# An expert layer in float32: the last weight tile split like the others, the final product moved from VectorE to GpSimd and ScalarE

## Chip, cores and metric

The kernel runs on one core of a Trainium2 chip. The metric is the device time of one execution in microseconds.

## What is computed

The program is one layer of a hybrid encoder in float32 for 2048 tokens of width 1024: a gated linear attention and a multi-head latent attention side by side, an output projection with residual, and then a mixture of 64 SwiGLU experts in 8 groups (one group per token, two experts of that group), with a final norm. The change touches the experts alone. Of the reference, that is:

```python
def expert_block(args):
    xb, e = args
    hdn = jax.nn.silu(xb @ w_gate[e]) * (xb @ w_up[e])
    return hdn @ w_down[e]
...
h = h + hier_moe(rmsnorm(h, ffn_norm[l]), ...)      # each token: two experts, weighted
return rmsnorm(h, final_norm)[:, N_META:]
```

Gate and up are 1024 x 512 for each expert, down is 512 x 1024: 6.3 MB of weights an expert, 403 MB in all.

## The kernel before

Up to about 1200 us the program makes the attention, the residual rows (kept in the output tensor) and the tables of the router. Then follow 64 blocks, one for each expert, taken so that neighbours belong to different groups. A block has room for 112 rows (tokens).

**Weights.** An expert's weights come as six tiles of 128 x 2048, 1 MB each: g0, g1 (gate), u0, u1 (up), d0, d1 (down). SP loads them into six raw buffers (`raw`). ScalarE (ACT) rounds a tile to `hi` in the matmul's reduced float32 (class `Weight`, `high`, line 1324), VectorE (DVE) takes `lo = raw - hi` (`low`, line 1330). There are four `hi` and four `lo` buffers, so a tile's `hi` and `lo` wait for the matmuls of the tile four places earlier. A product is then three matmuls (`mm3`, line 133): hi by hi, lo by hi, hi by lo. Five tiles go this way; the sixth, d1, is in `NATIVE` (line 44): it is used as plain float32 straight from `raw` (`down_whole`, line 1611), with a plain copy `hc` of its half of the hidden rows.

**One block on each engine,** by the names of the plan:
- TensorE (PE): `M_g0`, `M_g1`, `TH` (transposes of the hidden rows h of the block before), `M_u0`, `M_u1`, `TX0`, `TX1` (transposes of the next block's x), `M_d0`, `M_d1a`, `M_d1`.
- DVE: `lo_*`; `PROD`, the product h of silu(gate) and up; `HL` and `XL0`, `XL1`, the low parts of h and x; `Y0`, `Y1`, which add the down product in PSUM to the gathered base rows b and give z (two halves); `L`, the final product o = z * ss * g.
- ACT: `hi_*`; `HH`, `HC`, `XH0`, `XH1` (copies from PSUM); `SILU`; `SQ`, which squares z and sums to ss; `GM`, which makes the row g of norm weights.
- GpSimd (POOL): `GA` (gather of x for a later block), `GB` (gather of b, the rows' present values, from the output), `RT` (the root: two steps on ss, line 1651), `SO` (scatter of o to the output).

ss and g are such that a row's first visit leaves z as it is and its second visit normalizes it.

**Order.** `moe_plan` (line 1427) lays the order out with a list of operations, each with an engine, a cost in us and what it waits for; the order on each engine is then fixed. Gathers and scatters are indirect DMAs that POOL issues; weights are loaded by SP in the order in which the `hi` are planned. z has three buffers (`ZB`), b and o two each.

Of the kernel before, what the change touches and what calls it, by code (L numbers as in the profile page):

```python
# [8 lines left out]
F32 = mybir.dt.float32  # L9
# [3 lines left out]
AF = mybir.ActivationFunctionType  # L13
OP = mybir.AluOpType
# [4 lines left out]
P = 128  # L19
# [4 lines left out]
L = SEQ + META  # L24
# [267 lines left out]
def phase_g(tc, nc, a, zf, zv, hg, qd, qrd, kv, ident, ones, eps, z_rest, z_close, **_):  # L292
    late = ExitStack()
    with ExitStack() as ctx:
# [1132 lines left out]
def moe_plan():  # L1427


    W = 12 * 0.216  # L1430
    ops = {}

    def op(n, b, eng, cost, *deps):
        ops[n] = (b, eng, cost, deps)

    n = len(TILES)
    for i, t in enumerate(TILES):
        b, k = -(t[0] == "d"), i - HB
        old = ("M_" + TILES[k % n], -(k // n))
        op("hi_" + t, b, "A", 1.95, old)  # L1440
        op("lo_" + t, b, "V", 2.4, ("hi_" + t, 0), old)

    def ready(t):
        return [("lo_" + t, 0)] if t in TILES else []

    def cost(t):
        return W if t in TILES else W * 4 / 3

    for i, t in enumerate(("g0", "g1", "u0", "u1")):
        op("M_" + t, 0, "T", cost(t), *ready(t), *([(f"XL{i}", 1)] if i < 2 else []), *{0: [("PROD", 1)], 2: [("SILU", 1)]}.get(i, []))  # L1450
    op("M_d0", -1, "T", cost("d0"), *ready("d0"), ("HL", 0), ("Y0", 1), ("Y1", 1))
    op("M_d1a", -1, "T", cost("d1") / 2, *ready("d1"), ("HC", 0))
    op("M_d1", -1, "T", cost("d1") / 2, *ready("d1"), ("HC", 0))
    op("TH", -1, "T", 0.4, ("PROD", 1))
    op("HH", -1, "A", 0.43, ("TH", 0), ("M_d1", 2))
    if NATIVE:
        op("HC", -1, "A", 0.36, ("TH", 0), ("M_d1", 2))
    op("HL", -1, "V", 0.54, ("HH", 0), ("HC", 0))
    op("GA", 2, "G", 2.1, ("TX1", 0))
    op("GD", 2, "Q", 4.5, ("GA", 0))  # L1460
    for j in range(2):
        op(f"TX{j}", 1, "T", 0.4, ("GD", 1))
        op(f"XH{j}", 1, "A", 0.43, (f"TX{j}", 0), (f"M_u{j}", 0))
        op(f"XL{j}", 1, "V", 0.6, (f"XH{j}", 0))
        op(f"Y{j}", -1, "V", 0.7, (("M_d1a", "M_d1")[j], 0), ("Y0", 0) if j else ("BQ", 0), *([] if j else [("L", ZB)]))
    op("SILU", 0, "A", 0.68, ("M_g1", 0), ("PROD", 1))
    op("PROD", 0, "V", 0.72, ("M_u1", 0), ("SILU", 0), ("TH", 0))
    op("GB", -1, "G", 1.7, ("Y1", BB), ("OQ", 8))
    op("BQ", -1, "Q", 5.0, ("GB", 0))
    op("SQ", -1, "A", 1.3, ("Y1", 0), ("OQ", OB))  # L1470
    op("RT", -1, "G", 1.3, ("SQ", 0))
# [26 lines left out]
    late, t = {}, 0.0  # L1498
# [22 lines left out]
    while any(todo.values()):  # L1521
        best = None
        for k, v in todo.items():
            pick = None
            for q in v[:1 if k == "T" else 30]:
                if all(m in done for m in nodes[q][2]):
                    s = max([free[k]] + [done[m] + (LAG if nodes[m][0] != k else 0.07) for m in nodes[q][2]])
                    if k != "T":
                        s = max(s, late[q] - EARLY)
# [4 lines left out]
        s, q, k = best  # L1534
# [9 lines left out]
def phase_moe(tc, nc, a, ctx, ud, xlist, xexp, ident, ones, eps, rt, out, **_):  # L1544
    rp = rt["rp"]
    sp = ctx.enter_context(tc.tile_pool(name="e_s", bufs=2))
    p_g, p_t, xsb = rt["p_g"], rt["p_t"], rt["xs"]
    p_d = ctx.enter_context(tc.tile_pool(name="e_pd", bufs=2, space=PSUM))
    on = Ordered(tc)
    pools, made = rt["pools"], rt["made"]  # L1550
# [35 lines left out]
        on.scalar.activation(S.sg, S.p[0], AF.Silu, scale=S.rs)  # L1586

    def prod(S):
        S.h = sp.tile([BS, 4, P], F32, name="h", tag="h", bufs=1)
        on.vector.scalar_tensor_tensor(S.h.rearrange("s k p -> s p k"), S.p[1].rearrange("s (p k) -> s p k", k=4), S.grs,  # L1590
                                       S.sg.rearrange("s (p k) -> s p k", k=4), op0=OP.mult, op1=OP.mult)

    def turn(S):
        S.hn = 2 if NATIVE and S.e is not None else 4
        S.hh = sp.tile([P, 4, BS], F32R, name="hh", tag="hh", bufs=2)
        S.hl = sp.tile([P, 4, BS], F32R, name="hl", tag="hl", bufs=2)
        S.ph = p_t.tile([P, 4, BS], F32, name="pth", tag="t")
        for k in range(4):
            on.tensor.transpose(S.ph[:, k], S.h[:, k], ident[:BS, :BS])

    def hhi(S):
        on.scalar.copy(S.hh[:, :S.hn], S.ph[:, :S.hn])

    def hlo(S):
        on.vector.tensor_sub(S.hl[:, :S.hn], S.ph[:, :S.hn], S.hh[:, :S.hn].bitcast(F32))

    def hcopy(S):
        S.hc = sp.tile([P, 2, BS], F32, name="hc", tag="hc", bufs=2)
        on.scalar.copy(S.hc, S.ph[:, 2:])

    def down_whole(S, raw, hf):
        cs = slice(512 * hf, 512 * hf + 512)
        for k in range(2):
            on.tensor.matmul(S.d[hf], S.hc[:, k], raw[:, k, cs], start=False, stop=k == 1)
# [76 lines left out]

# [15 lines left out]
    for t in ("g0", "g1", "u0", "u1", "d0", "d1"):
        do["hi_" + t] = lambda S, g, t=t: hi(S, t, g)
# [6 lines left out]
    eng = {"T": on.tensor, "V": on.vector, "A": on.scalar, "G": on.gpsimd}  # L1715
# [23 lines left out]
    with tc.For_i(0, again, 1):  # L1739
        nx = nc.values_load(nxi[0:1, 0:1], min_val=0, max_val=NX)  # L1740
        with tc.For_i(0, nx, 1) as x:
# [8 lines left out]
            V = sp.tile([P, 2, NT, 4], F32, name="xV", tag="xV", bufs=1)  # L1750
# [8 lines left out]
            for k in range(2):  # L1759
                for t in range(NT):  # L1760
# [30 lines left out]
            for j in range(2):  # L1791
                w = Weight(nc, rp, *S.w["d", j]).high(rp, on.scalar).low(pools, 4 + j, on.vector).parts()
# [83 lines left out]
```

## Time and profile before

| | us |
|---|---|
| median of 3 runs (2433.43 to 2434.52) | 2434.23 |
| the profiled execution | 2433.11 |
| its span in the profile | 2431.1 |
| PE busy (share of the span) | 2343.4 (96%) |
| DVE busy | 1760.6 (72%) |
| ACT busy | 1385.0 (57%) |
| POOL busy | 831.3 (34%) |

Busy time is the time in which an engine's instructions ran, summed over the span. Matmuls are pipelined, so a PE that is busy throughout may still be waited for or wait a little; what a matmul takes is read from the distance between two starts. The three names `raw`, `hi` and `lo` in a row of the profile are the tiles above; `pg` and `pd` are the products in PSUM, `pt` and `pth` the transposes. Line 123 stands for every operation of the experts, as one helper records them all.

### The profile page before, as it was taken

To read this page: it belongs to the slowest core of one execution; us is meant where nothing else is said; L and a number is where in the kernel's file an instruction comes from. 1 tells how busy PE (TensorE), PEld (TensorE's weight loads), DVE (VectorE), ACT (ScalarE), POOL (GpSimd) and SP (SyncE) were. 2 spreads that over 40 slices of the span, in tenths; PEclk is the share of its full clock that TensorE was granted. 3 is DMA by queue.
4 is the path that set the end of the run, shared out by engine and by line. 5 is a ranking of instruction groups with operands and counts; after the bars stand their busy time and mean duration, and the time that the engine had idled before them with its cause. 6 is when DMAs were issued, how large, how long until landed. Compare 5 with 4: busy or idle time off the path is not lost. (4 is left out here: it accounts for less than half of the span.)

```text
span 2431.1 us, 35542 instructions
## 1 busy us (share of the span) xinstructions
PE 2343.4 (96%) x12897; PEld 1878.4 (77%) x12897; DVE 1760.6 (72%) x2755; ACT 1385.0 (57%) x2082; POOL 831.3 (34%) x676
## 2 busy tenths in 40 slices
PE   7999999899999999999699999999999999999997
PEld 7899997678789999989667767776777677777764
DVE  6334334677567676777778888888888888888885
ACT  5211103554356555555367777777777777777774
POOL 0000002622000212111234555555556545455553
PEclk9999999899999999999899999999999999999998
DMA  6212115555331212111599999999999999999994
GB/s 213 76 64 68 63 43 159 160 158 182 134 119 36 88 60 81 66 68 41 196 289 394 383 388 379 384 382 381 378 373 384 381 379 384 389 377 381 382 382 166
DMA packets 152960, 571.65 MB, mean 235 GB/s; under 512 B 28940, under 2 KB 71452, under 8 KB 103628
## 3 DMA queue, kind: packets, MB, share of 16 engines
q1 hardware_dynamic: 125612, 509.71, 56.5%
q0 software_dynamic: 24720, 50.91, 6.3%
q10 hardware_dynamic: 2448, 8.72, 1.2%
q8 instruction: 103, 1.69, 0.3%
q14 instruction: 77, 0.63, 0.1%
HBM read 529.71 MB, written 77.27 MB: 250 GB/s over the span
## 5 line engine op out<-in xcount | busy, mean ns | idle before, releaser
L123 DVE TENSOR_TENSOR lo<-raw,hi 128x2048 fp32r<-128x2048 f32 x317 | 720.7, 2285 | 67.5 <-ACT hi L123 61.7
L123 ACT CAST hi<-raw 128x2048 fp32r<-128x2048 f32 x318 | 607.6, 1911 | 275.1 <-PE pg L123 185.8
L123 PE MATMUL pg<-hi,xh 128*112 128x512 f32 x1024 | 434.3, 424 | 0.0
L123 PE MATMUL pg<-hi,xl 128*112 128x512 f32 x1024 | 407.6, 398 | 2.7 <-DVE xl L123 2.7
L123 PE MATMUL pg<-lo,xh 128*112 128x512 f32 x1024 | 401.8, 392 | 0.0
L123 POOL DMA_INDIRECT out_dram<-o,src x64 | 266.0, 4156 | 105.2 <-DVE hl L123 87.2
L123 POOL DMA_INDIRECT b<-out_dram,src x64 | 179.4, 2803 | 324.5 <-DVE z L123 324.0
L123 PEld LDWEIGHTS pg<-lo,xh 128*112 128x112 f32 x1024 | 180.5, 176 | 69.9 <-issue 15.1
L123 PEld LDWEIGHTS pg<-hi,xh 128*112 128x112 f32 x1024 | 179.4, 175 | 66.4 <-issue 13.9
L123 PE MATMUL pd<-raw,hc 128*112 128x512 f32 x512 | 230.1, 592 | 0.0
L123 PEld LDWEIGHTS pg<-hi,xl 128*112 128x112 f32 x1024 | 178.9, 175 | 61.8 <-DVE xl L123 3.3
L134 PE MATMUL ps<-uh,wh 128*128 128x256 f32 (+3 forms) x768 | 218.6, 285 | 0.9 <-ACT uh L222 0.9
L135 PE MATMUL ps<-ul,wh 128*128 128x256 f32 (+3 forms) x768 | 218.3, 284 | 0.0
L136 PE MATMUL ps<-uh,wl 128*128 128x256 f32 (+3 forms) x768 | 217.5, 283 | 0.0
L123 PEld LDWEIGHTS pd<-raw,hc 128*112 128x112 f32 x512 | 90.2, 176 | 103.8 <-issue 96.9
L134 PEld LDWEIGHTS ps<-uh,wh 128*128 128x128 f32 (+1 forms) x768 | 144.8, 189 | 1.6 <-ACT uh L222 1.3
L135 PEld LDWEIGHTS ps<-ul,wh 128*128 128x128 f32 (+1 forms) x768 | 144.7, 188 | 0.6 <-DVE ul L223 0.2
L136 PEld LDWEIGHTS ps<-uh,wl 128*128 128x128 f32 (+1 forms) x768 | 144.7, 188 | 0.1
L256 DVE COPY st<-ps 128x256 f32<-128x256 f32 (+1 forms) x64 | 27.0, 422 | 144.9 <-PE ps L136 144.9
L337 POOL TENSOR_SCALAR_AFFINE_SELECT mf<-ones 128x128 f32<-128x128 f32 x2 | 0.6, 302 | 378.8 <-PE ps L136 378.8
L123 DVE SCALAR_TENSOR_TENSOR o<-z,ss,g 112x1024 f32<-112x1024 f32 x64 | 82.2, 1284 | 55.6 <-POOL ss L123 53.2
L123 DVE TENSOR_TENSOR z<-pd,b 112x512 f32<-112x512 f32 x128 | 87.9, 686 | 45.3 <-PE pd L123 45.1
(2412 smaller groups left out, 5359.7 us busy)
## 6 DMA issues: line engine op xcount, KB each, us to landing
raw<-in_w_gate_dram SPq DMA_DIRECT2D x128, 1024.0 KB
raw<-in_w_up_dram SPq DMA_DIRECT2D x128, 1024.0 KB
raw<-in_w_down_dram SPq DMA_DIRECT2D x128, 1024.0 KB
x<-in_x_dram SPq DMA_DIRECT2D x32, 512.0 KB
zf<-st SPq DMA_DIRECT2D x85, 128.0 KB
hg<-x SPq DMA_DIRECT2D x16, 512.0 KB
x<-hg SPq DMA_DIRECT2D x16, 512.0 KB
out_dram<-x SPq DMA_DIRECT2D x16, 512.0 KB
```

Of the source, the lines that this page charges most:

```text
L123: return self.tc.keep_in_program_order(f(*args, **kw))
L134: nc.tensor.matmul(out, lh, rh, start=start, stop=False, **kw)
L135: nc.tensor.matmul(out, lh, rl, start=False, stop=False, **kw)
L136: nc.tensor.matmul(out, ll, rh, start=False, stop=stop, **kw)
L256: nc.vector.tensor_copy(st[:w, :n - o], ps[:w, :n - o])
L337: nc.gpsimd.affine_select(mf[:, :, hh], ob, pattern=[[CH, 2], [1, CH]], compare_op=OP.is_ge, fill=0.0, base=0, channel_multiplier=-1)
```

## The change

- `NATIVE` goes: d1 is split like the other tiles, its product is `mm3`, `hc` and `down_whole` go, and `HH` and `HL` take all four parts of h. `M_d1a` and `M_d1` wait for `lo_d1` and `HL`.
- h is kept as it is computed (112 x 512); the transposes of `TH` read it in steps of four, where before `PROD` wrote it in that order.
- The final product is in two: `ZG` on POOL multiplies g by z in place, `L` on ACT multiplies that by ss, a number for each row. In the last block DVE does it in one, as before.
- The plan has new costs; the due times of `L` and `SO` are later.

```diff
-NATIVE = ("d1",)
-TILES = tuple(t for t in ("g0", "g1", "u0", "u1", "d0", "d1") if t not in NATIVE)
+TILES = ("g0", "g1", "u0", "u1", "d0", "d1")
...
-    W = 12 * 0.216
+    W = 2.78
...
-    op("M_d1a", -1, "T", cost("d1") / 2, *ready("d1"), ("HC", 0))
-    op("M_d1", -1, "T", cost("d1") / 2, *ready("d1"), ("HC", 0))
+    op("M_d1a", -1, "T", cost("d1") / 2, *ready("d1"), ("HL", 0))
+    op("M_d1", -1, "T", cost("d1") / 2, *ready("d1"), ("HL", 0))
...
-    op("GB", -1, "G", 1.7, ("Y1", BB), ("OQ", 8))
+    op("GB", -1, "G", 2.6, ("Y1", BB), ("OQ", 8))
...
-    op("RT", -1, "G", 1.3, ("SQ", 0))
-    op("GM", -1, "A", 1.1, ("L", 2))
-    op("L", -1, "V", 1.3, ("RT", 0), ("GM", 0))
-    op("SO", -1, "G", 2.1, ("L", 0))
+    op("RT", -1, "G", 1.9, ("SQ", 0))
+    op("GM", -1, "A", 1.24, ("L", 2))
+    op("ZG", -1, "G", 2.1, ("Y1", 0), ("GM", 0))
+    op("L", -1, "A", 1.06, ("RT", 0), ("GM", 0), ("ZG", 0))
+    op("SO", -1, "G", 2.6, ("L", 0))
...
     def prod(S):
-        S.h = sp.tile([BS, 4, P], F32, name="h", tag="h", bufs=1)
-        on.vector.scalar_tensor_tensor(S.h.rearrange("s k p -> s p k"), S.p[1].rearrange("s (p k) -> s p k", k=4), S.grs,
-                                       S.sg.rearrange("s (p k) -> s p k", k=4), op0=OP.mult, op1=OP.mult)
+        S.h = sp.tile([BS, FE], F32, name="h", tag="h", bufs=1)
+        on.vector.scalar_tensor_tensor(S.h, S.p[1], S.grs, S.sg, op0=OP.mult, op1=OP.mult)
...
+    def weigh(S):
+        on.gpsimd.tensor_mul(S.g, S.g, S.z)
+
     def last_norm(S):
+        if S.i < NE - 1:
+            return on.scalar.activation(S.o, S.g, AF.Copy, scale=S.ss)
         on.vector.scalar_tensor_tensor(S.o, S.z, S.ss, S.g, op0=OP.mult, op1=OP.mult)
```

How this moves the instructions, in a block of the middle. On DVE, before, from behind the first z to the first xl (`lo0` is u0's, then u1, d0, g0, g1; `o` is L):

```order
L123 TENSOR_TENSOR lo0_17341<-raw_17306,hi_17308 128x2048
L123 TENSOR_TENSOR z_17326<-pd_17288,b_17244 112x512
L123 TENSOR_TENSOR lo1_17364<-raw_17318,hi_17320 128x2048
L123 TENSOR_TENSOR lo2_17376<-raw_17358,hi_17362 128x2048
L123 SCALAR_TENSOR_TENSOR o_17366<-z_17326,ss_17367,g_17343 112x1024
L123 TENSOR_TENSOR hl_17370<-pth_17371,hh_17369 128x224
L123 TENSOR_TENSOR lo3_17421<-raw_17400,hi_17402 128x2048
L123 TENSOR_TENSOR lo0_17455<-raw_17423,hi_17425 128x2048
L123 SCALAR_TENSOR_TENSOR h_17464<-pg_17378,grs_13958,sg_17453 112x128x4
L123 TENSOR_TENSOR xl_17428<-pt_17429,xh_17427 128x448
```

The same stretch of the changed kernel, from the lo of u0 on (then u1, d0, d1, g0, g1):

```order
L122 TENSOR_TENSOR lo2_17571<-raw_17537,hi_17539 128x2048
L122 TENSOR_TENSOR z_17569<-pd_17505,b_17457 112x512
L122 TENSOR_TENSOR lo3_17592<-raw_17565,hi_17567 128x2048
L122 TENSOR_TENSOR lo0_17618<-raw_17588,hi_17590 128x2048
L122 TENSOR_TENSOR lo1_17629<-raw_17624,hi_17626 128x2048
L122 TENSOR_TENSOR hl_17599<-pth_17600,hh_17598 128x448
L122 TENSOR_TENSOR lo2_17660<-raw_17645,hi_17647 128x2048
L122 SCALAR_TENSOR_TENSOR h_17688<-pg_17605,grs_13958,sg_17649 112x512
L122 TENSOR_TENSOR lo3_17691<-raw_17681,hi_17683 128x2048
L122 TENSOR_TENSOR xl_17653<-pt_17654,xh_17652 128x448
```

Between z and hl three `lo` now follow each other, where two and the final product stood; h stands between the `lo` of g0 and g1.

On POOL, before, a block from the root to the gather of b (`DMA` are the indirect ones: `out` SO, `xs` GA, `b` GB; a name in brackets is what is waited for):

```order
L123 TENSOR_SCALAR ss_20559<-ss_20559 112x1 [waits Activation_49]
L123 TENSOR_TENSOR ss_20559<-ss_20559,t_hx_14033 112x1 [waits Pool_49]
L123 DMA out_0_dram<-o_20558,src_6417 2048x1024 [waits DMASW5_49,DVE_49]
L123 DMA xs2_13832<-ud_73,src_6417 112x1024 [waits PE_49]
L123 DMA b_20892<-out_0_dram,src_6417 112x1024 [waits DMASW7_49,DMASW1_49,DVE_49]
```

And now:

```order
L122 DMA b_20228<-out_0_dram,src_6417 112x1024 [waits DMASW4_49,DMASW2_49,DVE_49]
L122 TENSOR_TENSOR g_20018<-g_20018,z_20014 112x1024 [waits Activation_49]
L122 TENSOR_SCALAR ss_20041<-ss_20041 112x1 [waits Activation_49]
L122 TENSOR_TENSOR ss_20041<-ss_20041,t_hx_14029 112x1 [waits Pool_49]
L122 DMA xs2_13832<-ud_73,src_6417 112x1024 [waits DMASW3_49,PE_49]
L122 DMA out_0_dram<-o_20040,src_6417 2048x1024 [waits Activation_49]
```

The product ZG (`g` by `z`) stands between the gather of b, which waits for the z before it on DVE, and the root; the gather of x is now ahead of the scatter.

On ACT, now, from `GM` on (`o,ss` from z is SQ, `o` from `g` and `ss` is L; the `hi` are d0, d1, g0, g1 and u0):

```order
L122 ACTIVATE g_18551<-gain_14086,t_first_14025,t_sec_14027 112x1024
L122 CAST hi_18568<-raw_18566 128x2048 [waits DMAHW1_49,DVE_49,PE_49]
L122 ACTIVATE o_18573,ss_18574<-z_18547 112x1024 [waits DMASW3_49,DVE_49]
L122 CAST hi_18604<-raw_18602 128x2048 [waits DMAHW2_49,PE_49,Activation_49]
L122 CAST hh_18576<-pth_18578 128x448 [waits PE_49]
L122 CAST hi_18625<-raw_18623 128x2048 [waits DMAHW3_49,PE_49,Activation_49]
L122 ACTIVATE sg_18627<-pg_18530,tab_6414 112x512
L122 ACTIVATE o_18573<-g_18551,ss_18574 112x1024 [waits Activation_49,Pool_49]
L122 CAST hi_18661<-raw_18659 128x2048 [waits DMAHW4_49,DVE_49,PE_49]
L122 CAST xh_18630<-pt_18632 128x448 [waits PE_49]
L122 CAST xh_18630<-pt_18633 128x448 [waits PE_49]
L122 CAST hi_18680<-raw_18678 128x2048 [waits DMAHW5_49,DVE_49,PE_49]
```

L stands ahead of the `hi` of g1 and waits for POOL.

## Rows read from the trace of the kernel before

**Rows 1.** Busy time by stage: us, PE, PEld, DVE, ACT, POOL, clock, DMA share, GB/s.
```profile
1800.00:2000.00 200.00, 200.00 (x863) 141.12 (x862) 173.32 (x131) 148.25 (x142) 110.79 (x54) 1.00 1.01 382
```
**Rows 2.** Groups of instructions by line: busy us, mean ns, idle before.
```profile
L123 ACT CAST hi<-raw 128x2048 fp32r<-128x2048 f32 x309 | 590.6, 1911 | 264.6 <-PE pg L123 175.3 <-DMA raw<-in_w_gate_dram 57.4 <-DMA raw<-in_w_up_dram 17.8
L123 ACT ACTIVATE o<-z 112x1024 f32<-112x1024 f32 x64 | 67.3, 1052 | 6.4 <-issue 6.4
...
L1177 POOL TENSOR_TENSOR x<-x,fge 128x1024 f32<-128x1024 f32 x14 | 33.5, 2390 | 85.0 <-PE pt L1162 72.7 <-PE pt__8088 L935 7.5 <-ACT qa L272 3.6
```
**Rows 3.** PE in order of time: start us, us, engine, operation.
```profile
1805.83 1.04 PE L123 MATMUL pt<-ident,xs 112*128 112x112 f32 x8
...
1809.46 3.60 PE L123 MATMUL pd<-raw,hc 128*112 128x512 f32 x8
...
1907.15 0.39 PE L123 MATMUL pg<-hi,xh 128*112 128x512 f32 x1
1907.38 0.39 PE L123 MATMUL pg<-lo,xh 128*112 128x512 f32 x1
```
**Rows 4.** DVE in order of time, one block of the expert stage.
```profile
1904.25 0.69 DVE L123 TENSOR_TENSOR z<-pd,b 112x512 f32<-112x512 f32 x1 [1.03 <-PE pd L123]
1904.86 2.28 DVE L123 TENSOR_TENSOR lo<-raw,hi 128x2048 fp32r<-128x2048 f32 x1
...
1907.66 2.28 DVE L123 TENSOR_TENSOR lo<-raw,hi 128x2048 fp32r<-128x2048 f32 x1
1910.68 2.29 DVE L123 TENSOR_TENSOR lo<-raw,hi 128x2048 fp32r<-128x2048 f32 x1 [0.74 <-ACT hi L123]
1913.76 1.29 DVE L123 SCALAR_TENSOR_TENSOR o<-z,ss,g 112x1024 f32<-112x1024 f32 x1 [0.79 <-POOL ss L123]
1914.96 0.38 DVE L123 TENSOR_TENSOR hl<-pth,hh 128x224 fp32r<-128x224 f32 x1
1915.26 4.48 DVE L123 TENSOR_TENSOR lo<-raw,hi 128x2048 fp32r<-128x2048 f32 x2
1919.66 1.16 DVE L123 SCALAR_TENSOR_TENSOR h<-pg,grs,sg 112x512 f32<-112x512 f32 x1
1920.65 1.15 DVE L123 TENSOR_TENSOR xl<-pt,xh 128x448 fp32r<-128x448 f32 x2
1922.81 0.69 DVE L123 TENSOR_TENSOR z<-pd,b 112x512 f32<-112x512 f32 x1 [1.01 <-PE pd L123]
```
**Rows 5.** POOL in order of time, the first from an earlier block.
```profile
1282.53 0.24 POOL L123 TENSOR_SCALAR ss<-ss 112x1 f32<-112x1 f32 x1
...
1908.01 2.79 POOL L123 DMA_INDIRECT b<-out_dram,src  x1 [4.57 <-DVE z L123]
1911.78 1.28 POOL L123 TENSOR_SCALAR ss<-ss 112x1 f32<-112x1 f32 x1 [0.98 <-ACT o L123]
1913.14 0.58 POOL L123 TENSOR_TENSOR ss<-ss,t_hx 112x1 f32<-112x1 f32 x1
1915.34 5.33 POOL L123 DMA_INDIRECT out_dram<-o,src  x1 [1.62 <-DVE hl L123]
1920.97 1.05 POOL L123 DMA_INDIRECT xs<-ud,src  x1 [0.30 <-issue]
```
**Rows 6.** DVE and POOL in order of time, before the expert stage.
```profile
1040.42 0.42 DVE L273 TENSOR_TENSOR ql<-qr,qh 128x256 fp32r<-128x256 f32 x1
1040.76 2.63 DVE L273 TENSOR_TENSOR qb__12397<-rr,qa 128x256 fp32r<-128x256 f32 x1
...
1040.73 2.39 POOL L1177 TENSOR_TENSOR x<-x,fge 128x1024 f32<-128x1024 f32 x1 [2.54 <-PE pt L1162]
```
**Rows 7.** A wait of PE in the first blocks: order of time, then busy by stretch.
```profile
1235.13 0.73 PE L123 MATMUL pg<-hi,xl 128*112 128x512 f32 x1 [2.69 <-DVE xl L123]
...
1232.44:1235.13 2.69, 0.00 (x1) 0.00 (x0) 2.69 (x5) 1.49 (x1) 1.96 (x1) 1.00 1.05 314
1235.13:1238.62 3.49, 3.48 (x8) 2.56 (x9) 3.41 (x7) 0.00 (x0) 0.00 (x0) 0.51 1.00 370
```

More of the change, by code (lines that the diff above doesn't have):

```diff
@@ L1439, in moe_plan @@
         old = ("M_" + TILES[k % n], -(k // n))
-        op("hi_" + t, b, "A", 1.95, old)
-        op("lo_" + t, b, "V", 2.4, ("hi_" + t, 0), old)
+        op("hi_" + t, b, "A", 1.92, old)
+        op("lo_" + t, b, "V", 2.3, ("hi_" + t, 0), old)
     def ready(t):
@@ L1446, in cost @@
     def cost(t):
-        return W if t in TILES else W * 4 / 3
+        return W
     for i, t in enumerate(("g0", "g1", "u0", "u1")):
@@ L1451, in moe_plan @@
     op("M_d0", -1, "T", cost("d0"), *ready("d0"), ("HL", 0), ("Y0", 1), ("Y1", 1))
-    op("M_d1a", -1, "T", cost("d1") / 2, *ready("d1"), ("HC", 0))
-    op("M_d1", -1, "T", cost("d1") / 2, *ready("d1"), ("HC", 0))
+    op("M_d1a", -1, "T", cost("d1") / 2, *ready("d1"), ("HL", 0))
+    op("M_d1", -1, "T", cost("d1") / 2, *ready("d1"), ("HL", 0))
     op("TH", -1, "T", 0.4, ("PROD", 1))
[L1455 to L1459, printed above, removed]
+    op("HH", -1, "A", 0.54, ("TH", 0), ("M_d1", 2))
+    op("HL", -1, "V", 0.62, ("HH", 0))
+    op("GA", 2, "G", 1.6, ("TX1", 0))
     op("GD", 2, "Q", 4.5, ("GA", 0))
     for j in range(2):
-        op(f"TX{j}", 1, "T", 0.4, ("GD", 1))
-        op(f"XH{j}", 1, "A", 0.43, (f"TX{j}", 0), (f"M_u{j}", 0))
-        op(f"XL{j}", 1, "V", 0.6, (f"XH{j}", 0))
+        op(f"TX{j}", 1, "T", 0.44, ("GD", 1))
+        op(f"XH{j}", 1, "A", 0.54, (f"TX{j}", 0), (f"M_u{j}", 0))
+        op(f"XL{j}", 1, "V", 0.62, (f"XH{j}", 0))
         op(f"Y{j}", -1, "V", 0.7, (("M_d1a", "M_d1")[j], 0), ("Y0", 0) if j else ("BQ", 0), *([] if j else [("L", ZB)]))
     op("SILU", 0, "A", 0.68, ("M_g1", 0), ("PROD", 1))
-    op("PROD", 0, "V", 0.72, ("M_u1", 0), ("SILU", 0), ("TH", 0))
-    op("GB", -1, "G", 1.7, ("Y1", BB), ("OQ", 8))
+    op("PROD", 0, "V", 0.8, ("M_u1", 0), ("SILU", 0), ("TH", 0))
+    op("GB", -1, "G", 2.6, ("Y1", BB), ("OQ", 8))
     op("BQ", -1, "Q", 5.0, ("GB", 0))
-    op("SQ", -1, "A", 1.3, ("Y1", 0), ("OQ", OB))
-    op("RT", -1, "G", 1.3, ("SQ", 0))
-    op("GM", -1, "A", 1.1, ("L", 2))
-    op("L", -1, "V", 1.3, ("RT", 0), ("GM", 0))
-    op("SO", -1, "G", 2.1, ("L", 0))
+    op("SQ", -1, "A", 1.25, ("Y1", 0), ("OQ", OB))
+    op("RT", -1, "G", 1.9, ("SQ", 0))
[3 more added lines that the diff above has]
+    op("SO", -1, "G", 2.6, ("L", 0))
     op("OQ", -1, "Q", 5.0, ("SO", 0))
@@ L1487, in moe_plan @@
                     eng, cost = "G", 4.46
+                if e + b == NE - 1:
+                    if n == "ZG":
+                        continue
+                    if n == "L":
+                        eng, cost = "V", 1.3
                 deps = [(m, e - d) for m, d in deps]
@@ L1512, in moe_plan @@
     for e in range(0, NE + 1):
-        for n, d in (("SQ", 3.0), ("L", 7.0), ("SO", 8.5)):
+        for n, d in (("SQ", 3.0), ("L", 9.0), ("SO", 10.2)):
             if (n, e) in nodes:
@@ L1588, in prod @@
     def prod(S):
-        S.h = sp.tile([BS, 4, P], F32, name="h", tag="h", bufs=1)
-        on.vector.scalar_tensor_tensor(S.h.rearrange("s k p -> s p k"), S.p[1].rearrange("s (p k) -> s p k", k=4), S.grs,
-                                       S.sg.rearrange("s (p k) -> s p k", k=4), op0=OP.mult, op1=OP.mult)
+        S.h = sp.tile([BS, FE], F32, name="h", tag="h", bufs=1)
+        on.vector.scalar_tensor_tensor(S.h, S.p[1], S.grs, S.sg, op0=OP.mult, op1=OP.mult)
     def turn(S):
-        S.hn = 2 if NATIVE and S.e is not None else 4
         S.hh = sp.tile([P, 4, BS], F32R, name="hh", tag="hh", bufs=2)
@@ L1597, in turn @@
         S.ph = p_t.tile([P, 4, BS], F32, name="pth", tag="t")
+        hv = S.h.rearrange("s (p k) -> s k p", k=4)
         for k in range(4):
-            on.tensor.transpose(S.ph[:, k], S.h[:, k], ident[:BS, :BS])
+            on.tensor.transpose(S.ph[:, k], hv[:, k], ident[:BS, :BS])
     def hhi(S):
-        on.scalar.copy(S.hh[:, :S.hn], S.ph[:, :S.hn])
+        on.scalar.copy(S.hh, S.ph)
     def hlo(S):
[L1605 to L1614, printed above, removed]
+        on.vector.tensor_sub(S.hl, S.ph, S.hh.bitcast(F32))
     def down(S, j, w, hf):
@@ L1684, in hi @@
         load(S, t)
-        if t == "d0" and NATIVE:
-            load(S, "d1")
         made[S.e, t].high(rp, eng)
@@ L1695, in mm_d @@
     def mm_d(S, j, hf):
-        if f"d{j}" in NATIVE:
-            w = made[S.e, f"d{j}"] if hf == 0 else made.pop((S.e, f"d{j}"))
-            return down_whole(S, w.view(w.raw), hf)
         w = made[S.e, f"d{j}"].parts() if hf == 0 else use(S, f"d{j}")
@@ L1702, in phase_moe @@
     do = {"GA": lambda S, g: gather(S.xs, S.src, ud), "SILU": lambda S, g: act(S), "PROD": lambda S, g: prod(S), "TH": lambda S, g: turn(S),
-          "HH": lambda S, g: hhi(S), "HL": lambda S, g: hlo(S), "HC": lambda S, g: hcopy(S),
+          "HH": lambda S, g: hhi(S), "HL": lambda S, g: hlo(S),
           "GB": lambda S, g: base(S), "SQ": lambda S, g: square(S), "RT": lambda S, g: root(S.ss, rt["hx"][:, S.e:S.e + 1]),
-          "GM": lambda S, g: blend(S), "L": lambda S, g: last_norm(S), "SO": lambda S, g: leave(S),
+          "GM": lambda S, g: blend(S), "ZG": lambda S, g: weigh(S), "L": lambda S, g: last_norm(S), "SO": lambda S, g: leave(S),
           "M_d0": lambda S, g: (mm_d(S, 0, 0), mm_d(S, 0, 1)), "M_d1a": lambda S, g: mm_d(S, 1, 0), "M_d1": lambda S, g: mm_d(S, 1, 1)}
```

## The prediction

> **What bounds the kernel now.** I read the busy time by stage first, then the order in time of PE, DVE and POOL inside one expert's block, then the lines of the operations that move. From 1250 us to the end the kernel goes through 64 blocks of one kind. In a 200 us stretch of it PE is busy for all 200, DVE for 173, ACT for 148, POOL for 111, and the loads keep the DMA engines full too (share 1.01) [rows 1]. The first z of a block starts at 1904.25 and the next one at 1922.81 [rows 4]: **a block takes 18.56 us**, and PE fills it. One split matmul starts 0.231 us after the other, a plain float32 one every (3.60 - 0.59) / 7 = 0.43 us [rows 3]. 60 x 0.231 + 8 x 0.43 = 17.3, and the remaining 1.3 are the twelve transposes (eight of them are listed with 1.04 [rows 3]). So PE sets the pace and the loads stand right behind it: I see no share to spare in them, and they are the same bytes after the change.
>
> The expert stage is about 62 such periods. The profiled execution took 2433.1 us, 1.1 less than the median of 2434.2; I sum against 2433.
>
> **The change, part by part.**
>
> *PE.* TH's transposes now read h in steps of four, as those of x do already, and I count no difference. The 4 plain matmuls of d1 (8 records) become 12 split ones: 8 x 0.43 = 3.44 goes, 12 x 0.231 = 2.77 comes. PE's work falls by 0.66 to 17.9 us a block. Alone that would be 62 x 0.66 = 41 us, if nothing else is longer.
>
> *DVE.* What counts is how long an operation keeps the next from starting. From the starts [rows 4]: lo 2.20 (a pair takes 4.48 for 2.28 each), z 0.61, L 1.20, hl 0.30, h 0.99, xl 0.53. Five lo, two z, L, hl, h, two xl: 11.0 + 1.2 + 1.2 + 0.3 + 1.0 + 1.1 = 15.8 us of the 18.56. After: a sixth lo (+2.2), L gone (-1.2), hl of twice the width (as xl, +0.23), h with plain strides (bounds: z's 0.61, the same shape, and today's 0.99; I take z's, -0.38). Sum 16.6 us. By count DVE fits below PE's 17.9.
>
> *ACT.* A sixth hi (1.91) and L (1.05, as the square of the same shape) come [rows 2]; the two small copies of h become one of twice the width, which I count as even. 148/200 x 18.56 = 13.7, and 16.7 after: it fits.
>
> *POOL.* It gains ZG, a product of two 112x1024 tiles that both lie in SBUF. The nearest row is the product of 128x1024 tiles in the layer before, 2.39 us, always alike [rows 2]; I take 2.3 for the time that it keeps others away. The bounds of what it costs DVE are 0 (it falls beside z, h, hl and xl, which read one operand from PSUM) and 2.3.
>
> **Why the sums don't decide.** DVE and POOL exclude each other when both read two tiles from SBUF. The trace shows it outside this stage: a DVE subtraction of 0.41 us takes 2.63 us when it starts beside that POOL product, and ends 0.27 after it [rows 6]. Inside the stage it shows from the other side: the first step of the root, 0.24 us alone, takes 1.28 when it starts under a lo, and ends with it [rows 5, 4]. An indirect DMA of POOL suffers more: 1.05 us when DVE is at xl; the gather of b, 2.79, ends 0.86 after the lo it met; the scatter that meets two lo without a gap between them takes 5.33, and ends 0.93 after the second [rows 5, 4]. Today this costs nothing, as POOL's results have time and DVE waits for the root anyway. After the change the order on POOL is gather of b, ZG, root, gather of x, scatter; on ACT the hi of the next g1 stands behind L, which waits for the root. So there is a ring from one z1 to the next, worked out with the starts above (z1 = 0):
> - lo u1 runs 0.6 to 2.9, lo d0 2.8 to 5.1. The gather of b asks at 0.95 and gets through 0.9 after the gap: 6.0.
> - lo d1 has gone off at 5.2, to 7.5. ZG waits for it, then holds the port to 9.8. The lo of g0, due at 8.0, waits, and runs 9.7 to 12.0.
> - The root's first step queues behind that lo: 12.25; its second, 0.58: 12.9.
> - L on ACT, 1.05 and the hand-over: 14.05. The hi of g1 after it: 15.9.
> - lo g1 (16.1, 2.2), two xl (1.06), z0 (0.6), lo u0 (2.2): the next z1 starts at **22.15 us**.
>
> In this ring PE waits some 4 us a block for xl. The trace has such a wait: 2.69 us for xl, and in the stretch behind it the granted clock is 0.51, the 1.2 of its two levels of 1.2 and 2.4 GHz, with matmuls 0.43 apart in place of 0.23 [rows 7]. Eight of M_g0's twelve come late by 0.2 each, 1.6 us; hi d0 waits for M_g0, so lo d0 no longer follows lo u1 without a gap, and the gather of b gets through at 3.8 in place of 6.0. Then: ZG waits for lo d0 (6.0), to 8.2; lo d1 8.15 to 10.45; root 11.35 (lo g0 has to wait only until 11.3); L 12.5; hi g1 14.35; lo g1 14.55; next z1 **20.6 us**. With 17.9 + 1.6 of work PE's wait is then short (1 us), the clock stays up in the next block, and the long form returns. **I forecast the two by turns, 21.3 us on average**: 62 x (21.3 - 18.56) = 170, less some 8 for the blocks at both ends, which have no full ring: 2433 + 162 = 2595 us. With one form alone it would be 2433 + 62 x 2.04 = 2560 or 2433 + 62 x 3.59 = 2656; that is this case's own range.
>
> The last block keeps L on DVE, and the few us at the end don't change. On SP the loads keep their order. The raw tile of d1 comes free after its lo and no longer after PE; as the loads have more time per block than now, I count nothing for it.
>
> **Rivals.**
> 1. *The indirect DMA isn't held back by lo* (2 in 10). Then the gather of b is over at 2.0, ZG waits for lo u1 only as far as it must, and DVE never waits long: 16.6 + 2.3 and about 0.6 behind the root, 19.5 us, 2433 + 62 x 0.94 = 2491; with the root's share hidden too, 19.1, 2466. Against it speak the scatters of 5.33 beside pairs of lo [rows 5]. The Trainium skill, SBUF — State Buffer, Who interferes with whom, holds that a `tensor_tensor` did not stall a DMA in its probe, since it takes only the read side of the shared port pair and writing descriptors needs the write side; by that page this rival would be the forecast, and the trace's 5.33 against 1.05 differs from it.
> 2. *Faster: the port doesn't decide* (14 in 100). If ZG falls beside z, h, hl and xl (3.9 us of DVE's block can cover it) or the product doesn't block a lo, the block goes down to PE's 17.9 or to what the loads allow. 2433 - 41 = 2392 if the loads can go faster; if they can't give more than half of it, 2413. The point from which it decides: DVE has 17.9 - 16.6 = 1.3 us to give, so less than that must be lost to ZG and the root, and the root must be there before ACT wants L. For it: sums by engine all fit. Against: three lo stand behind z1 in a row, which is where ZG becomes ready, and a blocked operation in rows 6 waits for the whole product.
> 3. *No change* (5 in 100): losses of about 2.0 us on DVE and no waiting for the root give 18.6.
> 4. *The long ring alone, or longer* (8 in 100): if the gap of 0.1 us before lo d1 is too short for the gather, it gets through after lo d1, and the block takes 22.9: 2433 + 62 x 4.3 = 2700.
> That the change does not do what it says I exclude: the rows of the order show ZG on POOL, L on ACT, six lo on DVE.
>
> **The numbers.** Forecast with its two forms 53 in 100, rival 1 20, rival 2 14, no change 5, rival 4 8. The range takes in the forecast and rival 1: from 2465 to 2670 us; some 22 in 100 is left out (rival 2, no change, part of rival 4). Measurements of this kernel tell about 0.2% (5 us) from no change. Faster by more than that: 0.14; within: 0.05; slower: 0.81.
>
> **What would show it.** Right: PE with idle time before M_g0, ended by DVE xl; lo with a spread of durations, up to 4.5 us where ZG is in front; ZG of more than 2.3 where a lo is in front; gathers of b of about 5 us; ACT idle before o (L), ended by POOL ss; a granted clock below 1.00 in the expert stage. Wrong: lo at 2.28 throughout (then ZG doesn't hold the port), gathers of b at 2.8 or less in every block (rival 1), PE without waits at 17.9 a block (rival 2).

## The result and the profile after

The changed kernel takes 2594.17 us (median of four runs, 2592.8 to 2599.95), the kernel before 2433.83 beside it: the ratio is 1.0665, with an interval of 1.0651 to 1.0678. The profiled execution after took 2593.7 us, its span is 2592.0.

The busy time of the same 200 us as in [rows 1] (us, PE, PEld, DVE, ACT, POOL, granted clock, DMA share, GB/s), after:

```profile
1800.00:2000.00 200.00, 182.63 (x796) 137.02 (x795) 183.75 (x117) 156.04 (x134) 136.94 (x55) 0.94 0.93 329
```

No engine is busy throughout now. PE, which filled the stretch before, idles for 17 us, the clock is granted at 0.94, and the loads fell from 382 to 329 GB/s. What waits for what, in the view of waits for the same stretch (engine and output waited with, releaser: us in total, times, longest):

```profile
POOL b L122 <- DVE z L122: 56.4, 10, 7.4
ACT o L122 <- POOL ss L122: 27.0, 9, 5.6
DVE lo L122 <- ACT hi L122: 19.1, 13, 3.1
PE pg L122 <- ACT xh L122: 11.1, 5, 2.4
PE pg L122 <- DVE xl L122: 8.3, 6, 1.7
```

From the second row down this is the ring that the prediction drew: L (written to o) on ACT waits for the root (ss), DVE's lo waits for the hi behind L, and PE waits for xh and xl. The groups by line, form by form, in the same stretch (busy us, mean ns, idle before and its releasers):

```profile
L122 DVE TENSOR_TENSOR lo<-raw,hi 128x2048 fp32r<-128x2048 f32 x59 | 155.7, 2657 | 19.3 <-ACT hi L122 19.1
...
L122 POOL DMA_INDIRECT b<-out_dram,src x10 | 52.3, 5231 | 56.4 <-DVE z L122 56.4
...
L122 POOL TENSOR_TENSOR g<-g,z 112x1024 f32<-112x1024 f32 x9 | 24.1, 2680 | 0.2
L122 POOL TENSOR_SCALAR ss<-ss 112x1 f32<-112x1 f32 x9 | 19.5, 2162 | 0.8
...
L122 ACT ACTIVATE o<-g,ss 112x1024 f32<-112x1024 f32 x9 | 10.4, 1152 | 27.0 <-POOL ss L122 27.0
```

A lo that took 2.28 us in [rows 4] averages 2.66, the gather of b went from 2.79 [rows 5] to 5.23, the root's first step from 1.28 to 2.16. Two blocks of POOL in order of time (start, us):

```profile
1910.27 7.21 POOL L122 DMA_INDIRECT b<-out_dram,src  x1 [3.87 <-DVE z L122]
1917.51 2.39 POOL L122 TENSOR_TENSOR g<-g,z 112x1024 f32<-112x1024 f32 x1
1919.98 2.17 POOL L122 TENSOR_SCALAR ss<-ss 112x1 f32<-112x1 f32 x1
1922.23 0.58 POOL L122 TENSOR_TENSOR ss<-ss,t_hx 112x1 f32<-112x1 f32 x1
...
1932.84 5.01 POOL L122 DMA_INDIRECT b<-out_dram,src  x1 [7.40 <-DVE z L122]
1937.88 2.42 POOL L122 TENSOR_TENSOR g<-g,z 112x1024 f32<-112x1024 f32 x1
```

and DVE in the same blocks:

```profile
1909.32 0.68 DVE L122 TENSOR_TENSOR z<-pd,b 112x512 f32<-112x512 f32 x1
1909.92 6.68 DVE L122 TENSOR_TENSOR lo<-raw,hi 128x2048 fp32r<-128x2048 f32 x3
1916.53 0.61 DVE L122 TENSOR_TENSOR hl<-pth,hh 128x448 fp32r<-128x448 f32 x1
1917.06 5.00 DVE L122 TENSOR_TENSOR lo<-raw,hi 128x2048 fp32r<-128x2048 f32 x1
...
1925.81 2.29 DVE L122 TENSOR_TENSOR lo<-raw,hi 128x2048 fp32r<-128x2048 f32 x1 [3.09 <-ACT hi L122]
...
1931.88 0.68 DVE L122 TENSOR_TENSOR z<-pd,b 112x512 f32<-112x512 f32 x1
1932.48 4.48 DVE L122 TENSOR_TENSOR lo<-raw,hi 128x2048 fp32r<-128x2048 f32 x2
1937.39 5.05 DVE L122 TENSOR_TENSOR lo<-raw,hi 128x2048 fp32r<-128x2048 f32 x1 [0.43 <-ACT hi L122]
```

The first block is a long one: three lo follow z1 without a gap, and the gather ends 0.88 us after the third. ZG runs from 1917.51 on, just as lo g0 has become due (1917.06), and that lo takes 5.00. The root's first step waits under that lo (2.17) and ends with it; lo g1 then waits 3.09 us for its hi. From z1 to z1 it is 1931.88 - 1909.32 = 22.56 us. In the next one a gap of 0.43 stands ahead of the third lo, and the gather gets through there, after 5.01.

Over 59 blocks, measured from z1 to z1, there are three kinds: 27 with a gather of 6.9 to 7.3 us, mean 22.57; 24 with one of 2.8, mean 19.82; 8 with one of 5.0, mean 20.98. No long block follows another. The mean is 21.24. What decides is seen on PE, in M_g0 ahead of the second block above, which is of the kind with 5.0 (start, us; the wait in brackets):

```profile
1926.26 0.48 PE L122 MATMUL pg<-hi,xh 128*112 128x512 f32 x1 [2.25 <-ACT xh L122]
...
1928.69 0.77 PE L122 MATMUL pg<-hi,xl 128*112 128x512 f32 x1 [1.72 <-DVE xl L122]
1929.26 0.63 PE L122 MATMUL pg<-hi,xh 128*112 128x512 f32 x1
1929.68 0.63 PE L122 MATMUL pg<-lo,xh 128*112 128x512 f32 x1
```

Behind the waits the matmuls start 0.43 apart, the lower of the clock's two levels (1.2 of 1.2 and 2.4 GHz; granted 0.59 over the 3.5 us from 1928.69 on). M_g0 ahead of each of the 24 short blocks has six to eight such slow steps, and the first matmul behind it starts 0.63 to 1.22 us after z1; ahead of all 27 long blocks there is none, and that matmul starts 0.28 to 0.80 us before z1. hi d0, which waits for M_g0, is then in time, and the three lo start 2.20 us apart, without any gap. The blocks with 5.0 lie between: four have five slow steps ahead of them, four none.

### The profile page after: what moved, and what is told of

It reads as the page before. It is cut to its first block, busy times and chain, and to the rows that moved or that the text cites. A ratio compares the mean times of both kernels' runs of the same rounds, so it can differ in the third digit from the quotient of the medians.

```text
span 2592.0 us, 36187 instructions
## 1 busy us (share of the span) xinstructions
PE 2381.5 (92%) x13153; PEld 1959.8 (76%) x13153; DVE 1959.9 (76%) x2756; ACT 1546.4 (60%) x2145; POOL 1090.4 (42%) x739
## 5 line engine op out<-in xcount | busy, mean ns | idle before, releaser
L122 DVE TENSOR_TENSOR lo<-raw,hi 128x2048 fp32r<-128x2048 f32 x381 | 1012.0, 2674 | 130.1 <-ACT hi L122 123.8
L122 ACT CAST hi<-raw 128x2048 fp32r<-128x2048 f32 x382 | 723.6, 1906 | 119.9 <-PE pg L122 56.5
L122 PE MATMUL pg<-hi,xl 128*112 128x512 f32 x1024 | 435.0, 425 | 55.7 <-DVE xl L122 55.7
L122 POOL DMA_INDIRECT b<-out_dram,src x64 | 314.7, 4918 | 348.5 <-DVE z L122 347.5
L122 PE MATMUL pg<-lo,xh 128*112 128x512 f32 x1024 | 423.8, 414 | 0.0
L122 PE MATMUL pd<-hi,hh 128*112 128x512 f32 x512 | 206.6, 404 | 1.2 <-DVE z L122 1.2
L122 PE MATMUL pd<-hi,hl 128*112 128x512 f32 x512 | 201.5, 394 | 1.2 <-DVE hl L122 1.2
L122 PE MATMUL pd<-lo,hh 128*112 128x512 f32 x512 | 201.8, 394 | 0.0
L122 ACT ACTIVATE o<-g,ss 112x1024 f32<-112x1024 f32 x63 | 72.6, 1152 | 202.7 <-POOL ss L122 202.7
L122 POOL TENSOR_TENSOR g<-g,z 112x1024 f32<-112x1024 f32 x63 | 176.4, 2799 | 20.0 <-DVE z L122 11.2
```

What stands on the lines that cost most here:

```text
L122: return self.tc.keep_in_program_order(f(*args, **kw))
```

## The experiments

The theory: between one z1 and the next stands a ring (GpSimd's gather, product and root, then L on ScalarE, then hi g1, lo g1, xl), and the shared port holds GpSimd's part of it back. Rivals: the sixth split itself costs the time; the product's hold on DVE's port is the whole loss; the two forms of the block have nothing to do with TensorE's clock.

### L behind hi g1

```
-    op("L", -1, "A", 1.06, ("RT", 0), ("GM", 0), ("ZG", 0))
+    op("L", -1, "A", 1.06, ("RT", 0), ("GM", 0), ("ZG", 0), ("hi_g1", -2))
```

> The changed kernel with L put behind hi g1 and the first xh on ScalarE: hi g1 no longer waits for the root. Ring theory: the ring is broken there; DVE's 16.6 and the 2.3 of ZG remain, 18.6 to 19.5 us a block, 2436 to 2490 us, and PE's waits for xl and xh nearly go. Rival (the loss is in the port, with or without the wait on ScalarE): 2560 to 2600.

Measured: 2451.11 us, ratio to before 1.0072 (1.0056 to 1.0089). **143 of the 160 us are back once L stands behind hi g1.** (The compiled order changed with it in two more places: on GpSimd the product stands ahead of the gather, of which more below; on DVE the first xl stands ahead of lo g1.) A block takes 18.88, DVE is busy nearly all of it, and no hi waits for a load. The busy time of 200 us of this kernel:

```profile
1900.00:2100.00 200.00, 193.26 (x890) 146.47 (x889) 199.26 (x129) 169.74 (x148) 158.38 (x66) 1.00 1.02 380
```

Its product and DVE's three lo in order of time:

```profile
1913.84 6.53 POOL L122 TENSOR_TENSOR g<-g,z 112x1024 f32<-112x1024 f32 x1 [3.22 <-DVE z L122]
...
1913.61 8.91 DVE L122 TENSOR_TENSOR lo<-raw,hi 128x2048 fp32r<-128x2048 f32 x3
```

The product waits under two lo and runs when the third is due; three lo that need 6.68 take 8.91. That is 2.2 us of DVE a block, the price of ZG in the prediction's sum (2.3): 16.6 + 2.3 = 18.9, measured 18.88.

### Half the product

The kernel above, with ZG over columns 512 to 1023 only, so that the first half of the columns goes out without the factor z. The gather is kept behind the product by a dependence.

```
...
-        on.gpsimd.tensor_mul(S.g, S.g, S.z)
+        rows.zg = getattr(rows, "zg", []) + [on.gpsimd.tensor_mul(S.g[:, 512:], S.g[:, 512:], S.z[:, 512:])]
```

> The kernel with L behind hi g1, with ZG over the second half of the columns only (512 of 1024; the first half of the rows goes out without the factor z). GpSimd keeps its order of that kernel: product, gather of b, root. Port theory (in that kernel DVE is busy all the time, and what the product holds of the port, 2.3 us a block, is paid in full by DVE): half the product gives back 1.1 to 1.2 us a block until the loads limit it at about 18.1 to 18.3, so 2405 to 2425 us. Rival (the 18.84 us a block come from the wait for the root or from the split, not from the product's hold): 2440 to 2455.

Measured: 2430.69 us, ratio 0.9983 (0.9974 to 0.9992), 20 us below the kernel with the whole product and 6 us above the upper end of what the port theory expected. The lo group shows the price, its mean 2.35 in place of 2.62 us, six times 0.27 = 1.6 us a block. That is more than half of 2.2; DVE now idles ahead of some lo, and part of the product may fall there. In time only 20.4 / 62 = 0.33 us a block came back: the blocks are uneven now (17.8 to 21.1 from z1 to z1), as ACT waits for the loads (DMA share 1.02 at 384 GB/s). So the price is seen in the rows, and in the time only a part of it.

### The product alone

The kernel before with ZG on GpSimd and L on ScalarE, and nothing else.

```
-    op("L", -1, "V", 1.3, ("RT", 0), ("GM", 0))
+    op("ZG", -1, "G", 2.1, ("Y1", 0), ("GM", 0))
+    op("L", -1, "A", 1.06, ("RT", 0), ("GM", 0), ("ZG", 0))
...
```

> The kernel before with the other part alone: ZG on GpSimd and L on ScalarE, d1 still unsplit, h in steps, the old figures in the plan. Ring theory: the ring needs no sixth lo, and with five lo DVE has 2.2 us less work, while ZG (2.3) and the root still stand between z1 and L: 18.6 to 20.5 us a block, 2436 to 2550 us, with PE waiting for xl behind hi g1 in part of the blocks. Rival (the split is what costs): no longer than before, 2420 to 2440.

Measured: 2620.35 us, ratio 1.0768 (1.075 to 1.0786), longer than the whole change. The plan puts L ahead of hi g0 here, one hi earlier. Waits over 1250 us of its expert stage:

```profile
DVE lo L123 <- ACT hi L123: 365.7, 60, 7.1
ACT o L123 <- POOL ss L123: 328.5, 58, 6.4
```

With five lo DVE waits some 6 us a block for hi. The loss comes without the split. The size that I gave (18.6 to 20.5 us a block) was too small: (2620 - 2434) / 62 + 18.57 = 21.6 us a block. I put that down to the ring, which closes one hi earlier; no run tests it.

### The split alone

d1 split, h in natural order, the new figures; no ZG, L on DVE as before.

```
-    op("ZG", -1, "G", 2.1, ("Y1", 0), ("GM", 0))
-    op("L", -1, "A", 1.06, ("RT", 0), ("GM", 0), ("ZG", 0))
+    op("L", -1, "V", 1.3, ("RT", 0), ("GM", 0))
...
```

> The change without its last part: the tile d1 is split whole, h is in natural order and the plan has the new figures, but there is no product on GpSimd (ZG), and the last norm L is one operation on DVE again, as before. Ring theory (POOL's product and the root hang between z1 and the next hi): no ring is left; DVE has six lo, 16.6 + 1.2 = 17.8 us a block, PE 17.9, so a block takes 17.9 to 18.8 us and the time is 2393 to 2450 us. Rival (the sixth split itself is what costs, by DVE's and ACT's added work): the time stays near the changed kernel's, 2560 to 2600.

Measured: 2708.48 us, ratio 1.1134 (1.1098 to 1.1171): the expectation was wrong, and more than the rival's time came out. The reason is in two rows of its waits over the expert stage:

```profile
DVE o L122 <- POOL ss L122: 238.2, 52, 6.7
...
POOL xs L122 <- PE pt L122: 154.6, 53, 14.7
```

I had counted DVE's work and not where L stands in it. The plan put L ahead of lo d1, and on GpSimd the root behind two transfers, of which the gather of x waits for PE; DVE stands still for 4.6 us at L in most blocks. So the next kernel puts L behind lo g1:

```
-    op("L", -1, "V", 1.3, ("RT", 0), ("GM", 0))
+    op("L", -1, "V", 1.3, ("RT", 0), ("GM", 0), ("lo_g1", -2))
```

> The split of d1 alone, as in the first experiment (no product on GpSimd, L one operation on DVE), but with L behind lo g1 and h on DVE, 12.8 us behind z1, where the root is long there. Theory (the first experiment's loss was DVE's wait for a root that stood behind two transfers, not the split): DVE 17.8, PE 17.9, no wait for the root; 17.9 to 18.5 us a block, 2393 to 2432 us, faster than the kernel before if the loads can go faster than 382 GB/s. Rival 1 (the loads are at their limit): 18.5 to 18.7, within 5 us of the kernel before. Rival 2 (six splits cost by themselves): 2560 and more.

Measured: 2451.05 us, ratio 1.0058 (1.004 to 1.0076). The theory's 2393 to 2432 and rival 1's 5 us were both missed: most blocks fell to 17.9 to 18.9, but two at the end took 24.4 and 34.1 (from TH to TH on PE). In the plan's order hi d0 and hi d1 of the last expert stood ahead of those of the experts before it, and ACT waited there for PE (8.54 us the longest). The same with the root ahead of the gather on GpSimd (the plan's line, and the dependence that is shown with the gather behind the root, below):

```
-    op("GB", -1, "G", 2.6, ("Y1", BB), ("OQ", 8))
+    op("GB", -1, "G", 2.6, ("Y1", BB), ("OQ", 8), ("RT", 2))
```

> As the kernel with L late on DVE, and on GpSimd the root ahead of the gather of b. If the root's lateness (behind a gather held by three lo) still reaches L at 12.8 us behind z1, this is faster than its neighbour by what L waited; if not, the two are alike within 5 us, since L has some 2 us to spare either way.

Measured: 2451.49, ratio 1.0069 (1.0052 to 1.0086): alike, so the root is in time for an L that stands late. Then the end was mended in the kernel with L late:

```
-EXTRA = {("lo_u0", 0): [("GA", -1)], ("lo_u0", 1): [("XL1", 0)]}
+EXTRA = {("lo_u0", 0): [("GA", -1)], ("lo_u0", 1): [("XL1", 0)], ("hi_d0", 64): [("hi_d1", 63)], ("hi_d1", 64): [("hi_d0", 64)]}
```

> The split of d1 with L late on DVE, and two order constraints for the last expert, whose hi d0 and hi d1 the plan had put ahead of the expert before (its last two blocks took 24.4 and 34.1 us in place of some 18.4). Theory: those 22 us are saved, 2425 to 2432 us; the other blocks stay at their 18.4 on average, against 18.57 before, and so the whole is 2 to 9 us faster than the kernel before, with the loads (386 GB/s, share 1.02) and not an engine at the limit. Rival (the long blocks at the end are the loads' backlog, not the order): 2445 to 2452 again.

Measured: 2424.99 us, ratio 0.9963 (0.995 to 0.9977), just below the range that was expected, and **0.4% faster than the kernel before** (its slowest run 2428.69, the fastest of the kernel before beside it 2431.92). Its busy time over the expert stage, and two of its waits:

```profile
1300.00:2360.00 1060.00, 1047.15 (x4839) 797.97 (x4838) 1037.64 (x749) 886.90 (x750) 712.41 (x287) 1.00 1.02 386
```

```profile
ACT hi L122 <- DMA raw<-in_w_up_dram: 34.0, 36, 2.3
ACT hi L122 <- DMA raw<-in_w_down_dram: 29.3, 40, 2.0
```

A block that doesn't wait takes 18.11 to 18.15, and the average is 18.40; ACT's waits for weight tiles are in the rows above, and the loads stand at 386 GB/s. The split, with L late and the end mended, is a gain of 10 us, and the other part of the change is the loss.

### The gather and the product on GpSimd

```
-BB = 2
+BB = 3
```

> The changed kernel with three buffers for the gathered rows b in place of two: the gather of b needn't wait for this block's z1 and leaves the ring. Ring theory: without the gather's wait behind three lo (7.2 us in the long blocks) ZG and the root come some 2 to 4 us earlier in each long block, 19 to 20 us a block, 2460 to 2525 us, and the gather's mean falls to about 2.8. Rival (what ZG itself takes from DVE through the port is the loss, the gather isn't): the time stays within 15 us of 2594.

Measured: 2595.38 us, ratio 1.0663 (1.0646 to 1.0681). This told nothing of the gather: with a third buffer the compiled order takes the gather one block earlier, and it again waits for the z1 that has just ended (mean 5.02 us, against 5.04 in the changed kernel). So the order was set by hand, by a dependence that puts the gather behind the root of two blocks before; the orders of the other engines are those of the changed kernel.

```
         o = gather(S.b, S.src, out)
+        if S.i > 2:
+            tc.add_manual_dep(o.ins, rows.roots[S.i - 2].ins.name, mybir.DependencyInfo(mybir.DependencyClass.NoSync, mybir.DependencyReason.DATA), reason="behind the root")
...
```

> The changed kernel with one thing moved: on GpSimd the gather of b stands behind the root (product, root, gather of b, gather of x, scatter) in place of ahead of the product; the other engines' orders are word for word those of the changed kernel, and L still stands ahead of hi g1. Theory A (what makes the long blocks is the gather, held back by lo's ahead of the product and the root): ZG then takes 6.5 us from z1 as in the kernel with L behind, the root is there at 9.3, hi g1 ends at 12.4, and DVE's own work sets the block: 18.7 to 19.2 us, 2440 to 2480 us, the gather's mean no longer matters. Theory B (L ahead of hi g1 on ScalarE is what costs, whatever stands first on GpSimd, as in the kernel with the product alone, which had the product first): 21 us or more, 2560 to 2620.

Measured: 2552.01 us, ratio 1.0475 (1.0457 to 1.0492), between the two theories. POOL in order of time:

```profile
1893.67 8.60 POOL L122 TENSOR_TENSOR g<-g,z 112x1024 f32<-112x1024 f32 x1
...
1915.09 6.52 POOL L122 TENSOR_TENSOR g<-g,z 112x1024 f32<-112x1024 f32 x1 [5.98 <-DVE z L122]
```

Whatever stands first on GpSimd behind z1 is held by the three lo: now the product of 2.4 us takes 8.60 or 6.52 (4.3 in the shortest blocks). The blocks are of two kinds again, 21.52 and 19.0 to 19.3. The gather's place is worth 42 us. The other 101 separate this kernel from the one with L behind hi g1, which has the product first too. I put them down to L's place; that kernel also has the gather ahead of the root on GpSimd and the first xl ahead of lo g1 on DVE, and no run takes these apart.

### Filling TensorE's wait

The last question is what makes the forms alternate. Ahead of each M_g0 some matmuls of the real kind go into the bank that the first real one overwrites; they add work that the output doesn't need. Ten first:

```
+FILL = 10
...
+            if n == 0 and S.i is not None and S.i > 2:
+                for k in range(FILL):
+                    on.tensor.matmul(S.p[0], B[S.i - 2].hh[:, k % 4], w[0][:, k % 4], start=True, stop=True)
```

> The changed kernel with ten filling matmuls (of the same kind as the real ones, into the bank that the first real one overwrites) ahead of each M_g0, so that TensorE works through 2.3 us of its wait. They add work that the output doesn't need. By-turns theory (the clock's fall after the wait makes M_g0 and hi d0 late, which opens the gap through which the next gather of b passes early): with the clock up the gap is gone, the long form of 22.6 us comes block after block, and the time goes up to 2640 to 2680 us. Rival (the forms have nothing to do with the clock): 2580 to 2610, since PE's 17.9 + 2.3 = 20.2 still fits under both forms' average; the granted clock rises in either case.

Measured: 2538.12 us, ratio 1.0426 (1.0409 to 1.0444): both expectations were wrong, and 2.3 us of useless work a block made the changed kernel 56 us faster. Every block is 20.31 long with a gather of 2.8. I had overlooked that the filling itself makes M_g0 late: hi d0 now waits 2.0 us a block for it, and lo d0 comes 1.9 us behind the end of lo u1. Hence five and eight.

> The same with eight (1.85 us; PE's work 19.8 us a block). Clock theory: as with five, 2630 to 2680, if M_g0 isn't delayed. If what the ten did was to delay M_g0 itself until lo d0 no longer follows lo u1 without a gap, eight lie near that point: steady blocks of 19.9 to 20.1 us, 2505 to 2535 us, with every gather of b at 2.8.

Measured: 2511.0 us, ratio 1.0319 (1.0302 to 1.0336). 19.5 to 20.1 a block from z1 to z1, 19.9 on average, PE busy throughout at clock 1.00, and in the steady blocks every gather at 2.8 (one at 2.5): the gap can be had with a small delay and without the clock's fall.

> The changed kernel with five filling matmuls (1.2 us, not needed for the output) ahead of each M_g0 in place of ten: they lie inside the wait of a long block (2.25 us for xh and 1.72 for xl) and so don't make M_g0 later, and PE's work stays at 19.1 us a block, below either form. If it is the clock's fall in that wait that makes M_g0 end late and opens the gap for the next gather, and the filling keeps the clock up, the long form comes block after block: 2630 to 2680 us, slower than the changed kernel. If the wait alone does it, whatever the clock, the two forms go on by turns: 2580 to 2605. If the filling still delays M_g0 where a block is short, the gap stays open as with ten: 2500 to 2550.

Measured: 2595.66 us, ratio 1.0668 (1.065 to 1.0686). By the time this is the second case, but the trace is a mixture that tells more. After a short block the five still make M_g0 a little late (gather of 5.0, 20.4 us); after a long one they lie within the wait, and now the clock falls in some and stays up in others. Two such stretches of 3.5 us, each from the first matmul behind the second wait on, are alike in what stands ahead of them: a long block, then a wait of 0.56 us for xh and one of 1.71 for xl. In the first the clock falls, in the second it doesn't (the figure behind POOL's is the granted clock):

```profile
1396.80:1400.30 3.50, 3.44 (x9) 2.52 (x10) 3.50 (x5) 2.74 (x2) 0.00 (x0) 0.54 0.81 281
1459.20:1462.70 3.50, 3.50 (x15) 2.71 (x16) 3.50 (x4) 3.50 (x3) 0.00 (x0) 1.00 0.86 269
```

and POOL's gathers on both sides of each:

```profile
1378.42 7.21 POOL L123 DMA_INDIRECT b<-out_dram,src  x1 [3.88 <-DVE z L123]
1401.01 2.80 POOL L123 DMA_INDIRECT b<-out_dram,src  x1 [7.41 <-DVE z L123]
...
1440.75 7.21 POOL L123 DMA_INDIRECT b<-out_dram,src  x1 [3.88 <-DVE z L123]
1463.34 7.21 POOL L123 DMA_INDIRECT b<-out_dram,src  x1 [7.41 <-DVE z L123]
```

Where the clock stays up the long form follows the long form, which happens nine times here and never in the changed kernel; where it falls, a block with a gather of 2.8 or 5.0 follows, 18 times. (One more long block, at the very end, is followed by one with 5.0 without a fall.) So in the changed kernel the clock's fall is what ends a long block's series, as predicted; a filled delay does the same.

## Why the prediction was right, point by point

**Total and mechanism.** 2595 was forecast, 2594.2 measured; 21.3 us a block as the average of two forms by turns, 21.24 measured. The form by turns, its cause and its links are in the rows: the idle time of o ended by ss, that of lo by hi, that of PE by xh and xl, ZG of up to 3.7 us and lo of up to 5.0. That the total fits to 1 us is luck in part: both forms were mis-sized, in opposite directions.

**The long form** was 22.15, measured 22.57. The step "the gather of b asks at 0.95 and gets through 0.9 after the gap: 6.0" was too early. The gap of 0.1 us ahead of lo d1 isn't there, as rival 4 had it, and the gather ends behind the third lo, at 8.2. But then ZG needn't wait at all (8.2 to 10.6), and the root is there at 13.5 in place of 12.9. That adds 0.4 us, not the 0.75 of rival 4. L took 1.15 in place of 1.05.

**The short form** was 20.6, measured 19.8 on average (19.3 to 20.1). The gather passes by 3.8 as predicted. The step "ZG waits for lo d0 (6.0), to 8.2" failed: lo d0 does not come as late as 3.8. In 14 of the 24 it is due at 3.3 to 3.4, ZG starts at 3.8 and lo d0 is the one that waits (5.0 us; 20.1 a block). In the other 10 lo d0 starts at 2.8 to 2.9, and ZG does wait for it, but only until 5.1 (19.4 a block). The errors of the two forms nearly cancel in the mean, and a third kind (gather 5.0, 21.0 us) that I did not have lies between them.

**Rival 1** (the indirect DMA isn't held back) falls: 7.21 us beside three lo in a row, 2.80 with a gap. The Trainium skill, SBUF — State Buffer, Who interferes with whom, infers that a `tensor_tensor` doesn't stall descriptor writing. The trace differs: the lo are such operations, and the gather behind them took 7.21 where the shortest indirect DMAs take 1.0.

**Rival 2** (faster, the port doesn't decide) had the right condition, "the root must be there before ACT wants L", and the runs show that even with that condition met the product costs DVE 2.2 us: 2451, not 2392 to 2413. Its other assumption, that the loads allow less than PE, fits the best version, in which ACT waits for weight tiles.

**PE** was sized 0.2 us too low: 18.11 to 18.15 us a block is what the split version takes where nothing waits, against 17.9 summed and 18.56 before [rows 4]. The fall is 0.4 us and not 0.66. In such a stretch of it PE is busy throughout and DVE for all but 0.6 us, so that it isn't shown which of the two sets the pace:

```profile
1282.00:1350.00 68.00, 68.00 (x316) 51.87 (x315) 67.37 (x51) 57.68 (x49) 53.77 (x20) 1.00 1.02 394
```

## What to carry to other kernels

Work moved from DVE to GpSimd wasn't free for DVE here, where both read two tiles from SBUF: L cost DVE 1.2 us, the product on GpSimd took 2.2 of DVE's time in its place, and the chain through GpSimd took as long as the row of DVE operations it queued behind. Before putting an operation that waits for another engine into an in-order queue, look at who stands behind it: moving L behind one hi regained 143 of 160 us here, with an order on GpSimd that came with it (to put the gather behind the product and the root, tried by itself, was worth 42). And judge the parts of a change apart, each with an order that suits it: here the half that was worth keeping was hidden behind the other, and in the first order tried it looked worse than both.

## What the runs showed that I had not expected

- A waiting GpSimd operation got no turn between DVE operations that followed each other without a gap: a product of 2.4 us took 8.60 behind three lo, 6.52 behind two. A gap let it in that is smaller than the profile shows. In all 27 long blocks the lo start 2.20 us apart. In the 24 blocks where the gather is through 2.8 us after it asked, the second starts 2.20 to 2.80 after the first, and in two of these it is 2.20 as well; there hi d0 ends 0.03 to 0.06 us before lo d0 is due, in the long blocks 0.8 us or more before.
- 1.85 us of useless matmuls a block made the changed kernel 83 us faster (2511.0 against 2594.2), by delaying TensorE until DVE's row of lo had a gap.
- A third buffer for b changed nothing (2595.4): the compiled order used it to issue the gather a block earlier, at the same bad moment.
